# A Strassen matmul with log-sum-exp: four column blocks with the operands' roles exchanged, 512 moving columns instead of 256

## The chip, the cores and the metric

The kernel runs on one core of a Trainium2 chip. The metric is the device time of one execution in microseconds (us). Four engines matter, TensorE (PE in the profile; PEld are its weight loads), VectorE (DVE), ScalarE (ACT) and GpSimd (POOL), and the DMA queues.

## The reference

```python
m, k, n = 1024, 4096, 4096          # a: m x k, b: k x n, float32, random
x = np.matmul(a, b)
return special.logsumexp(x, axis=-1).astype(np.float32)
```

## The kernel before

Everything is cast to float16 for TensorE. A is held transposed in SBUF (`aT`). B comes in eight column blocks of 512. Block 0 is multiplied plainly while A arrives. Every other block uses one level of Strassen's scheme (in Winograd's way): a block of B is four quarters b11, b12, b21, b22, and seven products replace eight. VectorE makes the sums of quarters, T1, T4 and T6 as new tiles, T3 and T7 in place:

```python
if what == "t1":   add(self.T1[:, lo:hi], b11, b22)
elif what == "t6": add(self.T6[:, lo:hi], b11, b12)
elif what == "t4": sub(self.T4[:, lo:hi], b21, b11)
elif what == "t7": add(b21, b21, b22)
else:              sub(b12, b12, b22)                 # t3
```

T1, T4 and T6 exist once each, so the next block's T1 can be made only when TensorE has done with this block's. A block is worked off in four groups q, each of 2 x 128 rows of A. The sums of A are stationary (128 x 128), B's are moving (256 columns), and each of the seven products is 16 matmuls:

```python
def product(c, lhs, rhs, start=False, k=(0, KP)):     # KP = 16
    for i in range(*k):
        nc.tensor.matmul(c, lhs(i), rhs(i), ...)      # lhs: A's side, 128x128; rhs: B's side, 256 columns

# one group; r0, r1 are two accumulator tiles of 512 f32; c11, c12 halves of r0, c21, c22 halves of r1
s = fix_pool.tile([P, 4, H], f32, tag="s")            # scratch, one buffer
x, e = s[:, 1::2], s[:, 0:2]
m1(c11, start=True); m5(c12)
nc.scalar.copy(out=e, in_=halves(r0))                 # "the copy of e"
m2(c21, start=True); m6(c22)
nc.scalar.copy(out=s[:, 2], in_=c21)
add(s[:, 2], s[:, 2], e[:, 1]); sub(s[:, 0], s[:, 2], e[:, 0])
for f in deferred: f()
# ... sums of B for the next block ...
m3(c12); nc.scalar.copy(out=x[:, 0], in_=c12)         # "the copy of x0"
m4(c21); nc.scalar.copy(out=x[:, 1], in_=c21)
m7(c11)
sub(x, x, s[:, 0::2]); add(c22, c22, x[:, 0]); add(c11, c11, x[:, 1])
maxima()                                              # VectorE: row maxima; ScalarE: exp with a running sum, later
```

The rows of the result lie on partitions here, so the maximum of a row is one VectorE reduction, and ScalarE's exp takes it as a bias and sums as it goes.

Of the kernel before, what the change touches and what calls it, by code (L numbers as in the profile page):

```python
# [13 lines left out]
def kernel(  # L14
# [6 lines left out]
    nc = tc.nc  # L21
    P = 128
    FD = 512
    H = FD // 2
    f32 = mybir.dt.float32
    f16 = mybir.dt.float16
    AX = mybir.AxisListType
    ALU = mybir.AluOpType
    AF = mybir.ActivationFunctionType
# [4 lines left out]
    MT, KT, NB = M // P, K // P, N // FD  # L34
    MP, KP = MT // 2, KT // 2
    G = 4
    GI = KP // G
# [5 lines left out]
    cst_pool = ctx.enter_context(tc.tile_pool(name="cst", bufs=1))  # L43
    bt_pool = ctx.enter_context(tc.tile_pool(name="btp", bufs=2 * G))
    fix_pool = ctx.enter_context(tc.tile_pool(name="fix", bufs=1))
# [3 lines left out]
    psum_pool = ctx.enter_context(  # L49
        tc.tile_pool(name="psum", bufs=8, space=bass.MemoryType.PSUM)  # L50
    )
# [6 lines left out]
            name=nc.get_next_instruction_name(),  # L58
# [6 lines left out]
    aT = cst_pool.tile([P, KP, 2, MP, 2, P], f16, name="aT")  # L65
    s1 = cst_pool.tile([P, KP, MP, P], f16, name="s1")
    s2 = cst_pool.tile([P, KP, MP, P], f16, name="s2")
    s5 = cst_pool.tile([P, KP, MP, P], f16, name="s5")
    tb = cst_pool.tile([P, 3, KP, H], f16, name="tb")
    stg_slots = tb.rearrange("p t (i j) n -> p (t i) (j n)", j=4)  # L70
    NSLOT = 3 * KP // 4
    ident = cst_pool.tile([P, P], f16, name="ident")
    negmax = cst_pool.tile([P, MT, NB + 1], f32, name="negmax")
    tsum = cst_pool.tile([P, MT, NB + 1], f32, name="tsum")

# [4 lines left out]
    def add(o, x, y):  # L80
        nc.vector.tensor_tensor(out=o, in0=x, in1=y, op=ALU.add)  # L81

    def sub(o, x, y):
        nc.vector.tensor_tensor(out=o, in0=x, in1=y, op=ALU.subtract)  # L84
# [41 lines left out]

    class Block:

        def __init__(self, nb, raw=None, sums=None):
            self.nb = nb  # L130
            self.raw = raw or [
                bt_pool.tile([P, GI, 2, FD], f16, name=f"b_{nb}_{g}", tag="bt")
                for g in range(G)
            ]
            self.T1, self.T4, self.T6 = sums or (tb[:, 0], tb[:, 1], tb[:, 2])

        def load(self, lo, hi):
            nc.gpsimd.dma_start(  # L138
                out=self.raw[lo // GI][:, lo % GI : lo % GI + hi - lo],
                in_=b_rows[:, lo:hi, :, ts(self.nb, FD)],  # L140
            )
# [6 lines left out]
        def b(self, i, kp, h):  # L148
            return self.raw[i // GI][:, i % GI, kp, ts(h, H)]

        def make(self, what, lo=None, hi=None):
            if lo is None:
                for g in range(G):
                    self.make(what, g * GI, (g + 1) * GI)
                return
            u = self.raw[lo // GI][:, lo % GI : lo % GI + hi - lo]
            b11, b12 = u[:, :, 0, 0:H], u[:, :, 0, H:FD]
            b21, b22 = u[:, :, 1, 0:H], u[:, :, 1, H:FD]
            if what == "t1":
                add(self.T1[:, lo:hi], b11, b22)  # L160
            elif what == "t6":
                add(self.T6[:, lo:hi], b11, b12)
            elif what == "t4":
                sub(self.T4[:, lo:hi], b21, b11)
            elif what == "t7":
                add(b21, b21, b22)
            else:
                sub(b12, b12, b22)
# [68 lines left out]
    def a_sums_late(r, q):  # L237
        a11, a12 = aT[:, r, 0, q, 0, :], aT[:, r, 1, q, 0, :]
        a21, a22 = aT[:, r, 0, q, 1, :], aT[:, r, 1, q, 1, :]
        sub(a21, a21, a11)  # L240
        sub(a12, a12, a22)
# [97 lines left out]
    deferred = []  # L339

    def flush():
        for f in pending:
            f()
        pending.clear()
# [4 lines left out]
    again0 = lambda: Block(0, sums=[wide(t[:, :, 0:2]) for t in (s1, s2, s5)])  # L349
    again1 = lambda: Block(1, raw=[wide(aT[:, ts(g, GI), :, 0:2]) for g in range(G)])  # L350
    plan = [(lambda: blk1, range(MP - 1))]
    plan += [(lambda nb=nb: Block(nb), range(MP)) for nb in range(2, NB)]
    plan += [(again0, [MP - 1]), (again1, [MP - 1])]

    blk, nxt = None, blk1
    for step, (_, qs) in enumerate(plan):
        blk, nxt = nxt, None
        nb = blk.nb
        more = step + 1 < len(plan)
        early = more and plan[step + 1][0] is again0  # L360
        if more:
            if plan[step + 1][0] is again1:
                nxt = last
            else:
                nxt = plan[step + 1][0]()
                if step == 1:
# [3 lines left out]
                        out=ident[0:1, 0:2], in_=aT[0:1, 0, 0, MP - 1, :, 0]  # L370
# [5 lines left out]
        if step == 0:  # L376
            KH = K // 2
            for h in range(2):
                a16 = dram_pool.tile([2, P, KH], f16, name=f"a16_{h}")
                for m in range(2):  # L380
                    nc.gpsimd.dma_start(out=a16[m], in_=a_m[MT - 2 + m, :, ts(h, KH)])
                for m in range(2):
                    nc.sync.dma_start_transpose(
                        aT[:, ts(h, KP // 2), :, MP - 1, m, :].rearrange("p i t c -> p (i t) c"),
                        a16[m],
                    )
        quads = {}
        for q in qs:
            joint = step == 0
# [4 lines left out]
            c11, c12 = r0[:, 0:H], r0[:, H:FD]  # L394
            c21, c22 = r1[:, 0:H], r1[:, H:FD]

            def product(c, lhs, rhs, start=False, k=(0, KP)):
                for i in range(*k):
                    nc.tensor.matmul(  # L399
                        c,  # L400
                        lhs(i),
                        rhs(i),
                        start=(start and i == 0),
                        stop=(i == KP - 1),
                        skip_group_check=True,
                    )
# [4 lines left out]
            if final:  # L411
                c22 = psum_pool.tile([P, FD], f32, name="c22", tag="ps")[:, 0:H]
            s = fix_pool.tile([P, 4, H], f32, name=f"s_{step}_{q}", tag="s")
            x, e = s[:, 1::2], s[:, 0:2]
            if final:
                e = fix_pool.tile([P, 2, H], f32, name="e_last", tag="e")
            if joint and q > 0:
                e = e_next
# [78 lines left out]
            if final:  # L497
# [28 lines left out]
                    out=w, in_=w, func=AF.Exp, bias=n0, scale=-1.0, accum_out=l0  # L526
# [44 lines left out]
            if step == 1 and q == 1:  # L571
                a_sums_early(slice(0, KP // 2), MP - 1)
                a_sums_late(slice(0, KP // 2), MP - 1)
            if early and q == 1:
                last = again1().load_all()

    nc.sync.dma_start(out=out.rearrange("(p mt) -> p mt", mt=MT), in_=lg)
# [30 lines left out]
```

## Time and profile before

| | before |
|---|---|
| median of 20 runs | 421.94 us (421.46 to 423.25) |
| profiled span | 421.2 us |
| TensorE busy | 413.7 us (98%) |
| one Strassen block (3 to 6) | 48.9 us |
| VectorE, ScalarE busy in such a block | 26.1 us, 12.2 us |

The page of the kernel before: the span, the busy time of each engine, and the chain of work that ended last, by engine.

```profile
span 421.2 us, 8528 instructions
...
PE 413.7 (98%) x3643; PEld 348.9 (83%) x3643; DVE 258.7 (61%) x573; ACT 109.9 (26%) x279; POOL 73.0 (17%) x115
...
PE 97%; DMA 1%; DVE 0%; ACT 0%; issue 0%; SPq 0%; ACTq 0%
```

TensorE is busy nearly throughout, and it is 97% of the chain that ended last. Whatever is won must be won there, and whatever makes TensorE wait is lost.

The table by stage of the kernel before: each row is a stretch in us, then its length, and the busy time of each engine with instruction counts. The first row is block 4; the second is the first group of block 7.

```profile
core 0: us, PE busy (x) PEld busy (x) DVE busy (x) ACT busy (x) POOL busy (x), PEclk, DMA share, GB/s
...
196.78:245.69 48.91, 48.91 (x451) 43.83 (x449) 26.13 (x49) 12.20 (x32) 3.96 (x6) 1.00 0.53 87
...
343.50:355.73 12.23, 12.23 (x114) 10.96 (x113) 10.15 (x19) 3.04 (x8) 2.49 (x3) 1.00 1.15 188
```

In block 4 TensorE works for all 48.91 us, VectorE for 26.13. A group takes 12.23 us: seven products of 1.75.

How long is a matmul? The timeline of TensorE, before: start, extent, then the instruction. The extents overlap, so one reads the distance of the starts. First groups of four matmuls of 512 columns (block 0), then groups of four of 256 (block 7):

```profile
59.40 1.03 PE L221 MATMUL acc_1_94<-b_3_86,aT 128*128 128x512 f16 x4
60.26 1.03 PE L221 MATMUL acc_0_95<-b_3_86,aT 128*128 128x512 f16 x4
```

```profile
350.32 0.60 PE L399 MATMUL acc_0_0_3927<-b_0_3379,aT 128*128 128x256 f16 x4
350.76 0.60 PE L399 MATMUL acc_0_0_3927<-b_1_3380,aT 128*128 128x256 f16 x4
```

Four matmuls of 512 columns start every 0.863 us, 215.7 ns each. Four of 256 take 0.436 us, 109.1 ns each. Two of 256 columns are 2.5 ns dearer than one of 512. The Trainium skill, "TensorE: Matmul & The Clock Gate", section "Wait — 56ns, not 53.3ns?", says the same: columns at 2.4 GHz, and about 2.5 ns per matmul on top. This trace agrees (215.7 and 109.1 ns).

The timeline of VectorE, before, gives the prices for what the change puts there:

```profile
195.79 0.68 DVE L84 TENSOR_TENSOR b_1_1760<-b_1_1760 128x1024 f16<-128x1024 f16 x1
196.40 0.68 DVE L84 TENSOR_TENSOR b_2_1761<-b_2_1761 128x1024 f16<-128x1024 f16 x1
```

Operations on 1024 f16 elements start 0.60 us apart.

### The profile page before, as it was taken

What the parts mean: (1) busy time and instruction counts of PE and PEld (TensorE: products, weight loads), DVE (VectorE), ACT (ScalarE), POOL (GpSimd) and SP (SyncE); (2) the same over time, 40 slices, a digit from 0 to 9 for tenths busy, and PEclk for the clock granted to TensorE, in tenths of its full rate; (3) what the DMA queues carried; (4) which work ended last, traced back from release to release, by engine and by line L of the source; (5) the groups of instructions that cost most, each with busy time, mean ns of one, the idle gap of its engine ahead of it and who ended that gap; (6) DMA issues with size and microseconds to landing.
All of it is one profiled execution on the core that took longest, in us unless ns stands there. A gap on an engine that the chain in (4) does not pass through costs nothing.

```text
span 421.2 us, 8528 instructions
## 1 busy us (share of the span) xinstructions
PE 413.7 (98%) x3643; PEld 348.9 (83%) x3643; DVE 258.7 (61%) x573; ACT 109.9 (26%) x279; POOL 73.0 (17%) x115
## 2 busy tenths in 40 slices
PE   7999999999999999999999999999999999999995
PEld 2555558888888888888888888888888888888885
DVE  2466688878647693257812694336832587299855
ACT  2222341132132222122222212222221222222124
POOL 7667753001010020003000030000200030120000
PEclk9999999999999999999999999999999999999999
DMA  9999999999999099102990079400990039899000
GB/s 186 200 204 203 203 206 206 207 207 214 192 200 211 7 177 207 17 2 35 207 159 2 2 115 208 80 2 2 183 207 11 2 56 207 138 186 207 9 2 1
DMA packets 57845, 53.37 MB, mean 127 GB/s; under 512 B 10192, under 2 KB 56912, under 8 KB 57808
## 3 DMA queue, kind: packets, MB, share of 16 engines
q0 software_dynamic: 48928, 49.95, 71.8%
q1 hardware_dynamic: 8880, 2.89, 3.5%
q8 instruction: 28, 0.46, 0.4%
q14 instruction: 9, 0.07, 0.1%
HBM read 100.66 MB, written 2.10 MB: 244 GB/s over the span
## 4 chain that ended last, share of the span: by engine, by line
PE 97%; DMA 1%; DVE 0%; ACT 0%; issue 0%; SPq 0%; ACTq 0%
PE acc_1_92 L221 2%; PE acc_0_91 L221 2%; PE acc_0_93 L221 2%; PE acc_1_0_1343 L399 2%; PE acc_1_0_765 L399 2%; PE acc_0_0_763 L399 2%; PE acc_3_0_4335 L399 2%; PE acc_3_0_2691 L399 2%; PE acc_0_0_3927 L399 2%; PE acc_1_0_3515 L399 2%; PE acc_2_0_3103 L399 2%; PE acc_3_0_1611 L399 2%; PE acc_0_0_3387 L399 2%; PE acc_1_0_2975 L399 2%; PE acc_0_0_2307 L399 2%; PE acc_3_0_2151 L399 2%
## 5 line engine op out<-in xcount | busy, mean ns | idle before, releaser
L399 PEld LDWEIGHTS <-aT 128*128 128x128 f16 x1856 | 181.6, 98 | 21.1
L399 PEld LDWEIGHTS <-s_71 128*128 128x128 f16 x464 | 45.4, 98 | 5.5
L399 PEld LDWEIGHTS <-s_73 128*128 128x128 f16 x464 | 45.4, 98 | 5.3
L399 PEld LDWEIGHTS <-s_72 128*128 128x128 f16 x464 | 45.4, 98 | 5.3
L221 PEld LDWEIGHTS <-aT 128*128 128x128 f16 x192 | 16.7, 98 | 16.0 <-DVE aT L214 2.9
L192 POOL DMA_DIRECT2D tb<-in_a_dram x47 | 25.4, 543 | 7.0 <-issue 2.1
L203 PEld LDWEIGHTS <-tb 128*128 128x128 f16 x192 | 15.0, 100 | 12.3 <-DVE tb L296 1.0
L216 ACT COPY aT<-tps_98 128x512 f16<-128x512 f16 x24 | 14.1, 586 | 38.3 <-PE tps_98 L203 38.3
L214 DVE COPY aT<-tps_97 128x512 f16<-128x512 f16 x24 | 10.2, 424 | 19.0 <-PE tps_97 L203 19.0
L84 DVE TENSOR_TENSOR aT<-aT 128x256 f16<-128x256 f16 (+1 forms) x56 | 16.1, 339 | 0.0
L203 PE MATMUL tps_97<-ident,tb 128*128 128x128 f16 x96 | 9.5, 223 | 0.1
L203 PE MATMUL tps_98<-ident,tb 128*128 128x128 f16 x96 | 9.5, 223 | 0.0
L81 DVE TENSOR_TENSOR s_71<-aT 128x256 f16<-128x256 f16 (+1 forms) x26 | 8.1, 313 | 2.2 <-ACT aT L216 2.2
L138 POOL DMA_DIRECT2D b_0_2299<-in_b_dram x1 | 0.9, 878 | 45.9 <-PE acc_3_0_2151 L399 45.9
L138 POOL DMA_DIRECT2D b_0_3379<-in_b_dram x1 | 0.9, 878 | 45.7 <-PE acc_3_0_3231 L399 45.7
L138 POOL DMA_DIRECT2D b_0_3919<-in_b_dram x1 | 0.9, 878 | 45.1 <-PE acc_3_0_3771 L399 45.1
L138 POOL DMA_DIRECT2D b_0_2839<-in_b_dram x1 | 0.9, 890 | 45.0 <-PE acc_3_0_2691 L399 45.0
L81 DVE TENSOR_TENSOR s_72<-aT 128x256 f16<-128x256 f16 (+1 forms) x26 | 8.1, 313 | 0.0
L81 DVE TENSOR_TENSOR s_73<-aT 128x256 f16<-128x256 f16 (+1 forms) x26 | 8.1, 313 | 0.0
L138 POOL DMA_DIRECT2D aT<-in_b_dram x4 | 3.5, 897 | 21.5 <-PE acc_1_0_4055 L399 21.5
L282 PE MATMUL acc_1_96<-s_73 128*128 128x512 f16 x11 | 5.2, 608 | 1.2 <-DVE s_73 L285 1.2
L81 DVE TENSOR_TENSOR tb<-aT 128x1024 f16<-128x1024 f16 x8 | 5.2, 686 | 1.5 <-DMA aT<-in_b_dram 1.5
(1050 smaller groups left out, 891.7 us busy)
## 6 DMA issues: line engine op xcount, KB each, us to landing
tb<-in_a_dram POOLq DMA_DIRECT2D x47, 128.0 KB, 5.9
aT<-in_b_dram POOLq DMA_DIRECT2D x4, 1024.0 KB, 15.2
b_1_84<-in_b_dram POOLq DMA_DIRECT2D x4, 256.0 KB, 6.5
b_2_85<-in_b_dram POOLq DMA_DIRECT2D x4, 256.0 KB, 6.2
b_3_86<-in_b_dram POOLq DMA_DIRECT2D x4, 256.0 KB, 6.2
b_0_87<-in_b_dram POOLq DMA_DIRECT2D x2, 512.0 KB, 8.6
b_1_88<-in_b_dram POOLq DMA_DIRECT2D x2, 512.0 KB, 11.8
b_2_89<-in_b_dram POOLq DMA_DIRECT2D x2, 512.0 KB, 15.2
```

The costliest lines, as they stand in the source:

```text
L81: nc.vector.tensor_tensor(out=o, in0=x, in1=y, op=ALU.add)
L84: nc.vector.tensor_tensor(out=o, in0=x, in1=y, op=ALU.subtract)
L138: nc.gpsimd.dma_start(out=self.raw[lo // GI][:, lo % GI : lo % GI + hi - lo], in_=b_rows[:, lo:hi, :, ts(self.nb, FD)],)
L192: nc.gpsimd.dma_start(out=slot, in_=a_m[m, :, k0 * P : (k0 + kn) * P])
L203: nc.tensor.matmul(pst[:, ts(j, P)], src[:, ts(j, P)], ident, is_transpose=True, start=(j == 0), stop=(j == kn - 1),)
L214: nc.vector.tensor_copy(out=dst, in_=v)
L216: nc.scalar.copy(out=dst, in_=v)
L221: nc.tensor.matmul(pt, aT[:, i, kp, m // 2, m % 2, :], blk0.raw[i // GI][:, i % GI, kp, :], start=(done[m] == 0), stop=(done[m] == KT - 1),)
L282: nc.tensor.matmul(acc[2][1], zeros[:, 0:P], zeros[:, 0:FD], start=True, stop=True)
L399: nc.tensor.matmul(c, lhs(i), rhs(i), start=(start and i == 0), stop=(i == KP - 1), skip_group_check=True,)
```

## The change: its intent, and the diff

Blocks 3 to 6 exchange the roles: 128 columns of B's sums are stationary, and A's sums for 4 x 128 rows move, 512 columns in one matmul. A block is then two halves of 7 x 16 matmuls, not four groups of 7 x 16, so the fixed cost per matmul is paid half as often. The price is that products come out transposed: columns of the result lie on partitions, rows along the free axis. VectorE therefore turns squares of 32 x 32, takes maxima over 32 columns, subtracts them, ScalarE takes the exp, and VectorE sums. At the end GpSimd spreads the four partition groups' results into the four columns of `negmax` and `tsum` that these blocks would have filled.

```diff
+    slots = tb[:, 1, KP // 2 : KP] ...            # two scratch tiles in the unused half of T4
+    def lse_turned(c, slot, h, r):
+        nc.vector.transpose(out=slot, in_=c)
+        nc.vector.tensor_reduce(out=nm, in_=v, axis=AX.X, op=ALU.max, negate=True)
+        add(v, v, nm.unsqueeze(-1).broadcast_to((P, WN // 2, 32)))
+        nc.scalar.activation(out=slot, in_=slot, func=AF.Exp)
+        return lambda: nc.vector.tensor_reduce(out=tts[...], in_=v, axis=AX.X, op=ALU.add)
+    def merge_turned():                            # 7 small operations, one of them an exp on ScalarE
+    ...
+    def wide_step(blk, nxt):
+        for nt in range(2):
+            last = not nxt.wide and nt == 1
+            ...                                    # mk: sums for the next half, full size if last
+            product(c11, T1, s1); product(c12, b22, s5); product(c21, b11, s2)
+            nc.vector.tensor_copy(out=s[:, 1], in_=c12)
+            add(s[:, 1], s[:, 1], c21)
+            sub(s[:, 0], s[:, 1], c11)
+            for f in deferred: f()                 # end11 and merge_turned of the half before
+            mk("t1")
+            product(c22, T6, aT); mk("t6"); mk("t3")
+            product(c12, b12, aT)
+            sub(s[:, 0], c12, s[:, 0]); add(c22, c22, s[:, 0])
+            end12 = lse_turned(c12, slots[0], 1, 0)
+            end22 = lse_turned(c22, slots[1], 1, 1)
+            product(c21, T4, aT)
+            sub(s[:, 1], c21, s[:, 1])
+            end12(); end21 = lse_turned(c21, slots[0], 0, 1); end22()
+            for what in ("t4", "t7"):              # if last: only the first two quarters here
+                mk(what)
+            product(c11, b21, aT)
+            add(c11, c11, s[:, 1])
+            end11 = lse_turned(c11, e, 0, 0); end21()
+            if last: ...                           # the other two quarters of t4, t7
+            deferred.extend([end11, merge_turned])
...
+        if blk.wide:
+            wide_step(blk, nxt)
+            continue
...
+                spread_turned()                    # 32 small GpSimd copies, in block 7
                 last = again1().load_all()
```

## The prediction

> **What bounds the kernel now.** TensorE. The page gives PE 413.7 of 421.2 us (98%), and the chain of waits is 97% PE. The table by stage shows column blocks 3 to 6 at 48.9 us each, with TensorE busy throughout, VectorE 26.1 us (53%) and ScalarE 12.2 us. In the chain, 16 matmuls of 256 columns take 1.745 us, 109.1 ns each. In the timeline of the first block, four of 512 columns take 0.863 us, 215.7 ns each. That fits the Trainium skill, "TensorE: Matmul & The Clock Gate", section "Wait — 56ns, not 53.3ns?": columns at 2.4 GHz plus about 2.5 ns per matmul.
>
> **Removed from TensorE.** Each of the four blocks goes from 448 matmuls of 256 columns to 224 of 512: 896 x (2 x 109.1 - 215.7) = 2.2 us. That is the whole gain, 0.5%, all on the critical path. Weight loads (98 ns) stay hidden.
>
> **Added on VectorE.** ScalarE's copies and its summing exp move here. I price with starts in the VectorE timeline: 1024 f16 or 512 f32 elements 0.60 us back to back, 256 cycles 0.334 us (0.067 us fixed), about 0.12 us more when the operation reads its predecessor's result. For each half block (TensorE needs 112 x 215.7 ns = 24.2 us):
> - 20 block sums at half size, 0.334 each: 6.7
> - copy, add, sub of the first products and four combines: 4.7
> - four squares turned (transpose, max, subtract): 4 x 2.04 = 8.2. I take the transpose as one element per cycle (skill, "Vector Engine (DVE) Microarchitecture Reference", section 3.8); no trace here shows one yet.
> - four final sums: 2.4
> - merge, seven small operations with a trip to ScalarE: 1.75
>
> Estimate: 23.7 us of 24.2, against about 13 before. VectorE goes to 95-100% in these blocks. TensorE has 2 to 4 us of slack there (tightest: the copy of the second product before its bank is used again), so little or no stall.
>
> **Where I expect the loss: leaving the wide blocks.** The last half of block 6 makes full-size sums for block 7 (5.3 us more) with VectorE already full and about 10 us behind. Block 7's first group reuses the scratch tile, which frees only when VectorE's last combine is done. ScalarE, in order, first runs the last exp, then copies; only then may TensorE write that bank again; T4 and T7 arrive late too. By my sum TensorE stalls 4 to 8 us there. After that VectorE recovers. The 32 tiny POOL copies, 0.1 to 0.3 us each, precede block 1's reload, and may cost 0 to 2 us.
>
> **Sum.** 421.7 - 2.2 + 5 (exit) + 0.5 (rest) = 425 us. Range 418 to 437. Chances: faster by over 2% 0.01, within 2% 0.78, slower by over 2% 0.21.
>
> **What would show it.**
> - Timeline: 512-column matmuls 215.7 ns apart in blocks 3 to 6, four blocks at about 193.3 us instead of 195.6.
> - Table by stage: VectorE over 90% there; before, 53%.
> - Groups: transpose of 128x512 f32 near 0.7 us. Wrong if over 1 us.
> - Waits: one TensorE gap of several us at the start of block 7, released by ScalarE's copy or a VectorE sum; hardly any between wide halves.
> - The end after block 7 costs as before, within 2 us.
>
> **What would make it wrong.** A transpose at half rate adds some 2 us per half, ending near 435 to 440. If dependent VectorE steps cost less than priced, VectorE is not behind at the exit, the stall shrinks to 1 or 2 us, and the time is 420 to 421. A moving operand in four pieces of 128 columns could stream slower; I assume not.

## The result, and the profile after

The changed kernel takes 427.82 us in the median of 10 runs (426.82 to 428.94), against 421.94. The ratio is 1.0137, 95% interval 1.0126 to 1.0148: 1.4% slower. (Ratios are the mean time of one kernel's runs over that of the other's of the same rounds, so not quite the ratio of the medians.) The result is correct.

The page after: span, busy times, TensorE's busy tenths and its granted clock in 40 slices, and the chain.

```profile
span 426.6 us, 6832 instructions
...
PE 413.0 (97%) x2747; PEld 261.3 (61%) x2747; DVE 338.3 (79%) x773; ACT 83.3 (20%) x191; POOL 79.1 (19%) x149
...
PE   7999999999999999999999999999999958999996
...
PEclk9999999999999999999999999999999996999999
...
PE 88%; DVE 6%; DMA 4%; ACT 1%; issue 0%; SPq 0%; ACTq 0%
```

TensorE's busy time is almost what it was, but one slice shows 5 and its neighbour 8, and the clock falls to 6 tenths in the second of them. Those slices are the start of block 7.

The table by stage after (columns as above): block 4, the first group of block 7, and the piece of it that follows TensorE's wait.

```profile
195.19:243.53 48.34, 48.34 (x225) 21.94 (x224) 45.85 (x99) 5.65 (x11) 3.96 (x5) 1.00 0.54 89
...
340.23:361.41 21.18, 15.20 (x114) 12.39 (x113) 18.17 (x34) 4.18 (x9) 4.12 (x18) 0.84 1.18 196
353.19:359.66 6.47, 6.46 (x34) 4.71 (x34) 4.40 (x13) 0.77 (x3) 1.29 (x9) 0.55 1.24 207
```

A wide block takes 48.34 us where 48.91 stood, with TensorE busy throughout. Four of them take 193.39 us instead of 195.63, that is 2.24 less. VectorE is busy for 45.85 of 48.34 us, 95%. The first group of block 7 takes 21.18 us where 12.23 stood: 8.95 more. In the part behind TensorE's wait the granted clock is 0.55. (Block 3, the first wide one, has VectorE busy for only 39.3 us, 81%.)

So in the profiles: 2.24 won in the wide blocks, 8.95 lost at the exit, and 1.04 less before block 2 starts (97.85 against 98.89 us), in a part that the change hardly touches and whose length differs from run to run; the end after that group takes 65.19 against 65.47 us. Together 5.4, the difference of the two spans.

The waits of TensorE after, with their total, count and longest in us: the only one over 1.2.

```profile
PE acc_0_0_3173 L528 <- ACT s_0_3175 L595: 6.0, 1, 6.0
```

L595 is the copy of `e`. The timeline of TensorE around it:

```profile
345.30 1.91 PE L528 MATMUL acc_0_1_3174<-tb,aT 128*128 128x256 f16 x16
353.19 1.01 PE L528 MATMUL acc_0_0_3173<-b_0_2813,aT 128*128 128x256 f16 x4 [5.98 <-ACT s_0_3175 L595]
...
356.56 3.10 PE L528 MATMUL acc_0_1_3174<-tb,aT 128*128 128x256 f16 x16
359.50 0.60 PE L528 MATMUL acc_0_0_3173<-b_0_2813,aT 128*128 128x256 f16 x4
...
361.24 1.91 PE L528 MATMUL acc_1_0_3307<-tb,s_71 128*128 128x256 f16 x16
```

The product m3 (at 353.19) starts 6.0 us after m6, the product before it, has ended. Then its 16 matmuls take 3.37 us (353.19 to 356.56), where 16 took 1.75 before: half the speed, through m3 and most of m4. At 359.50, with m7, the speed is back. These two products take 6.31 us instead of 3.49: 2.82 us, besides the 5.98 of the wait.

The timeline of VectorE at the exit:

```profile
349.06 0.69 DVE L86 TENSOR_TENSOR wide_1_0_2993<-wide_1_0_2993,sw_1_2997 128x512 f32<-128x512 f32 x1
...
351.26 0.69 DVE L86 TENSOR_TENSOR ew_1_3155<-ew_1_3155,ident 128x512 f32<-128x512 f32 x1
...
354.39 0.69 DVE L86 TENSOR_TENSOR b_3_2816<-b_3_2816 128x1024 f16<-128x1024 f16 x1
354.99 0.42 DVE L86 TENSOR_TENSOR s_0_3175<-s_0_3175 128x256 f32<-128x256 f32 x1
```

The add at 349.06 is the last combine of block 6 (it frees the scratch tile), the one at 351.26 the last subtraction ahead of ScalarE's last exp. The line at 354.39 finishes T7; T4 was finished just before. At 354.99 comes VectorE's first add of block 7, which before came 8.2 us after the block's start (351.72 against 343.50); the block began at 340.2, so it now comes 14.8 after.

The timeline of ScalarE at the exit:

```profile
352.04 0.63 ACT L381 ACTIVATE ew_1_3155<-ew_1_3155 128x512 f32<-128x512 f32 x1 [5.24 <-DVE ew_1_3155 L86]
352.58 0.57 ACT L595 COPY s_0_3175<-acc_0_0_3173 128x512 f32<-128x512 f32 x1
...
356.96 0.28 ACT L391 ACTIVATE ident<-ident 128x96 f32<-128x96 f32 x1 [3.54 <-DVE ident L89]
357.15 0.35 ACT L670 COPY s_0_3175<-acc_0_0_3173 128x256 f32<-128x256 f32 x1
```

ScalarE works in program order: the exp of block 6's last square (352.04), then the copy of `e` (352.58), which sets m3 free. Later the exp of the merge (356.96), then the copy of x0 (357.15).

Inside the wide blocks there is no TensorE gap. The timeline of VectorE there, with its only wait of a half for TensorE, and a transpose:

```profile
229.76 0.69 DVE L86 TENSOR_TENSOR sw_1_2293<-sw_1_2293,wide_1_2_2291 128x512 f32<-128x512 f32 x1 [0.41 <-PE wide_1_2_2291 L427]
...
240.70 0.71 DVE L378 STREAM_TRANSPOSE tb<-wide_1_3_2292 128x512 f32<-128x512 f32 x1
```

VectorE waits 0.41 us for the third product in a half of 24.2 us. The transpose of 128 x 512 f32 takes 0.71 us.

### The profile page after: what moved, and what is told of

It is laid out like the page before. It is cut to its first block, busy times and chain, and to the rows that moved or that the text cites. A ratio compares the mean times of both kernels' runs of the same rounds, so it can differ in the third digit from the quotient of the medians.

```text
span 426.6 us, 6832 instructions
## 1 busy us (share of the span) xinstructions
PE 413.0 (97%) x2747; PEld 261.3 (61%) x2747; DVE 338.3 (79%) x773; ACT 83.3 (20%) x191; POOL 79.1 (19%) x149
## 4 chain that ended last, share of the span: by engine, by line
PE 88%; DVE 6%; DMA 4%; ACT 1%; issue 0%; SPq 0%; ACTq 0%
DMA tb<-in_a_dram 3%; PE acc_1_0_1347 L528 2%; PE acc_1_0_767 L528 2%; PE acc_0_0_765 L528 2%; PE acc_2_0_3483 L528 2%; PE acc_2_0_1482 L528 2%; PE acc_1_0_3307 L528 2%; PE acc_3_0_3755 L528 2%; PE acc_3_0_3619 L528 2%; PE acc_3_0_1615 L528 2%; PE acc_0_0_1215 L528 2%; PE acc_2_0_769 L528 2%; PE wide_0_1_2822 L427 2%; PE wide_1_2_2643 L427 2%; PE wide_0_0_2469 L427 2%; PE wide_1_1_2290 L427 2%
## 5 line engine op out<-in xcount | busy, mean ns | idle before, releaser
L528 PEld LDWEIGHTS <-aT 128*128 128x128 f16 x832 | 82.8, 100 | 17.1 <-issue 6.2
L427 PEld LDWEIGHTS <-tb 128*128 128x128 f16 x384 | 37.6, 98 | 45.1
L381 ACT ACTIVATE tb<-tb 128x512 f32<-128x512 f32 x24 | 15.1, 630 | 110.4 <-DVE tb L86 110.4
L234 PEld LDWEIGHTS <-aT 128*128 128x128 f16 x192 | 16.6, 98 | 14.4 <-DVE aT L227 1.8
L216 PEld LDWEIGHTS <-tb 128*128 128x128 f16 x192 | 13.9, 98 | 14.3 <-DMA tb<-in_a_dram 6.2
L528 PEld LDWEIGHTS <-s_71 128*128 128x128 f16 x208 | 20.4, 98 | 2.8
L528 PEld LDWEIGHTS <-s_73 128*128 128x128 f16 x208 | 20.4, 98 | 2.3
L528 PEld LDWEIGHTS <-s_72 128*128 128x128 f16 x208 | 20.3, 98 | 2.4
L86 DVE TENSOR_TENSOR tb<-tb,ident 128x512 f32<-128x512 f32 x24 | 16.6, 692 | 0.8
L379 DVE TENSOR_REDUCE ident<-tb 128x16 f32<-128x512 f32 x24 | 16.5, 686 | 0.9
L382 DVE TENSOR_REDUCE tts<-tb 128x16 f32<-128x512 f32 x24 | 16.2, 677 | 0.0
L86 DVE TENSOR_TENSOR s_71<-aT 128x256 f16<-128x256 f16 (+1 forms) x26 | 8.1, 313 | 2.1 <-ACT aT L229 1.5
```

What stands on the lines that cost most here:

```text
L86: nc.vector.tensor_tensor(out=o, in0=x, in1=y, op=ALU.add)
L216: nc.tensor.matmul(pst[:, ts(j, P)], src[:, ts(j, P)], ident, is_transpose=True, start=(j == 0), stop=(j == kn - 1),)
L234: nc.tensor.matmul(pt, aT[:, i, kp, m // 2, m % 2, :], blk0.raw[i // GI][:, i % GI, kp, :], start=(done[m] == 0), stop=(done[m] == KT - 1),)
L379: nc.vector.tensor_reduce(out=nm, in_=v, axis=AX.X, op=ALU.max, negate=True)
L381: nc.scalar.activation(out=slot, in_=slot, func=AF.Exp)
L382: return lambda: nc.vector.tensor_reduce(out=tts[:, 1 + h, ts(r, WN // 2)], in_=v, axis=AX.X, op=ALU.add)
```

## The experiments

The theory (A): VectorE is so full in the wide blocks that it enters block 7 with a queue; TensorE waits there, once, for what the queue holds back; the lowered clock is a consequence of that wait. Rivals: the loss belongs to the wide blocks themselves; or one single dependence makes it. "First group" below is from the first matmul of the first group behind the wide blocks to the first of the next group, from the profile of that run; 12.23 us before.

| run | median us | ratio to before, 95% | first group us |
|---|---|---|---|
| the change | 427.82 | 1.0137 (1.0126 to 1.0148) | 21.2 |
| e1_warm | 426.91 | 1.0111 (1.0095 to 1.0127) | 19.2 |
| e2_order | 426.20 | 1.0094 (1.0079 to 1.0109) | 19.3 |
| e3_scratch | 427.52 | 1.0144 (1.0106 to 1.0181) | 21.2 |
| e4_both | 428.10 | 1.0147 (1.0124 to 1.0170) | 20.6 |
| e11_order_and_merge | 425.25 | 1.0067 (1.0052 to 1.0083) | 17.6 |
| e7_two_together | 428.49 | 1.0154 (1.0140 to 1.0168) | 20.2 |
| e6_two_apart | 437.66 | 1.0361 (1.0344 to 1.0379) | 21.0 and 20.9 |
| e8_dose_inside | 428.60 | 1.0150 (1.0134 to 1.0165) | 21.0 |
| e10_dose_inside_big | 431.57 | 1.0221 (1.0205 to 1.0236) | 23.3 |
| e9_dose_exit | 430.43 | 1.0197 (1.0182 to 1.0213) | 22.4 |
| e5_late_squares | 419.76 | 0.9943 (0.9930 to 0.9955) | 12.2 |

All were correct. e1 to e4 ran on one chip, e5 to e11 on another, each beside its own runs of the kernel before (422.0 and 422.1 us).

### e1_warm: does the clock drop come from the idle time?

```diff
+            if nb == NB - 1 and q == 0:
+                idle = psum_pool.tile([P, FD], f32, name="idle", tag="ps")
+                for _ in range(24):                   # 512 columns each, result unused
+                    nc.tensor.matmul(idle..., aT[:, 0, 0, 0, 0, :], s1[:, 0], start=True, stop=True)
             m3(c12)
```

> 24 idle 512-column matmuls (24 x 215.7 ns = 5.2 us) are put where TensorE waits at the start of block 7. Theory A (the wait is set by VectorE's queue and ScalarE's order; the clock drop after it is a consequence of the idle time): the third product of block 7 still starts about 13.1 us after the block's start, since the fillers end before that; but the two products after the gap run at 109 ns per matmul and not 184 to 210, so block 7's first group takes about 18.2 us and not 21.2, and the run is 2.5 to 3 us shorter than the changed kernel: about 425. Rival B (those two products are slow for another cause, late sums or a busy memory): the time stays at 427.8, within 0.6.

Measured: 426.91 us. The timeline of TensorE in this run (fillers, m3, m4, m7):

```profile
347.29 5.34 PE L672 MATMUL idle<-s,aT 128*128 128x512 f16 x24
353.44 1.91 PE L528 MATMUL acc<-b,aT 128*128 128x256 f16 x16 [0.81 <-ACT s L595]
355.18 1.91 PE L528 MATMUL acc<-tb,aT 128*128 128x256 f16 x16
357.80 1.91 PE L528 MATMUL acc<-b,aT 128*128 128x256 f16 x16 [0.71 <-ACT s L680]
```

With the array kept busy, m3 still starts 13.1 us into the block, but runs at full speed (1.74 us from 353.44 to 355.18), and the granted clock of the whole run is 1.000 against 0.992. So the clock drop was a consequence of idle time: this half of the expectation held. The size was missed: about 1 us was saved, not 2.5 to 3. The last product shows why. It stands behind a new wait, 0.71 us, for a copy by ScalarE. ScalarE's timeline in this run:

```profile
357.20 0.28 ACT L391 ACTIVATE ident<-ident 128x96 f32<-128x96 f32 x1 [3.54 <-DVE ident L89]
357.39 0.35 ACT L680 COPY s<-acc 128x256 f32<-128x256 f32 x1
```

The copy of x0 (357.39) stands behind the exp of the merge (357.20), which waits for VectorE's queue. In the changed kernel the slow products had hidden this wait. The Trainium skill, "TensorE: Matmul & The Clock Gate", section "HAM oscillation — how this bites in real kernels", describes the drop: idle time longer than a window of about 3.4 us halves the clock until TensorE has been busy for a while. The 6.0 us wait of the changed kernel and the doubled durations after it agree; e2's wait of 3.3 us lies at the edge, and e4 below does not fit.

### e2_order and e3_scratch: which link holds m3?

Two edits, each alone. e2 issues ScalarE's last exp of block 6 behind the copies of block 7:

```diff
-        nc.scalar.activation(out=slot, in_=slot, func=AF.Exp)
+        exp = lambda: nc.scalar.activation(out=slot, in_=slot, func=AF.Exp)
+        if later is not None: later.append(exp)      # later = deferred, for the last square only
+        else: exp()
```

> Only ScalarE's last exp of block 6 is issued after the two copies of block 7. Theory A, with the exp ahead of the copy as the link that ends last: the copy now starts when the scratch tile comes free, about 9.6 us into block 7 and not 12.4, so TensorE's first gap falls from 6.0 to about 3.2 us; then it waits again for T4's and T7's last quarters (VectorE finishes them about 14.9 us into the block): the group takes about 16.5 us if the clock stays full, 18 to 19 if it drops; the run is 423 to 425.5. Rival (scratch tile or T4 and T7 alone set the gap): no change, 427.8 within 0.6.

e3 makes VectorE's last combine of block 6 earlier, so that the scratch tile comes free sooner:

```diff
             sub(s[:, 1], c21, s[:, 1])
+            if last:
+                product(c11, ...)
+                add(c11, c11, s[:, 1])
             end12()
```

> Only VectorE's last combine of block 6, which frees the scratch tile, is moved ahead of the third square: the tile comes free some 5.5 us sooner. Theory A: ScalarE's last exp still stands ahead of the copy, so TensorE's gap stays 6.0 us within 0.6 and the run 427.8 within 0.7. Rival (the scratch tile sets the gap): gap near zero, a wait for T4 instead, and 423 to 425.

Measured: e3 changed nothing (427.52 us, TensorE's wait 6.0 us, first group 21.2): the scratch tile alone was not what ended last. (Its profile is of the one execution of four that took 430.70 us; block 7 starts 2.4 us later there than in the change, so that excess lies before it.) e2 shortened the first wait from 6.0 to 3.3 us, as expected, but 3.3 us still brought the slow clock for the whole of m3, and a second wait of 1.8 us came behind m4. TensorE's timeline (m3 and m7):

```profile
350.36 3.57 PE L532 MATMUL acc<-b,aT 128*128 128x256 f16 x16 [3.27 <-ACT s L599]
...
357.44 1.91 PE L532 MATMUL acc<-b,aT 128*128 128x256 f16 x16 [1.77 <-ACT s L674]
```

Its 426.20 us is above the 423 to 425.5 expected: I had the link to m3 right. The second wait was not the one for T4 and T7 that I expected: m4 did not wait, and m7 waited for the copy of x0, a link that I had not seen.

### e4_both

Both edits together.

> Both of the former together. Theory A: TensorE's gap before the third product vanishes, and a gap of 3.5 to 4 us before the second half of the fourth product takes its place, since T4's last two quarters wait for the third and fourth squares (their memory is the squares' scratch): 422.5 to 423.5 if the clock stays full, up to 425.5 if it drops. Rival (only ScalarE's order or the tile counted): 419 to 420.

Measured: 428.10 us, no better than the change alone, and outside what either theory had said. TensorE's timeline (m3, first and second half of m4, m7, the next group):

```profile
348.54 1.91 PE L536 MATMUL acc<-b,aT 128*128 128x256 f16 x16 [0.92 <-DVE tb L89]
350.28 1.04 PE L536 MATMUL acc<-tb,aT 128*128 128x256 f16 x8
353.80 1.80 PE L536 MATMUL acc<-tb,aT 128*128 128x256 f16 x8 [2.48 <-DVE tb L89]
358.03 3.21 PE L536 MATMUL acc<-b,aT 128*128 128x256 f16 x16 [2.43 <-ACT s L678]
361.07 1.91 PE L536 MATMUL acc<-tb,s 128*128 128x256 f16 x16
```

The first wait is down to 0.92 us, where none was expected, and the one for T4 is there (2.48 us, where 3.5 to 4 was expected). But m7 again waits for the copy of x0 (2.43 us) and starts 17.6 us into the block, against 17.5 in e1 and e2. In all these versions m7 starts where VectorE's queue and the merge let it. Worse, the clock dropped, though no single wait was longer than 2.5 us. The second half of m4, behind waits of 0.92 and 2.48 us, has an extent of 1.80 us for 8 matmuls where its first half has 1.04; the granted clock there is 0.51. The same happens in m7 behind the third wait (3.04 us for 16, from 358.03 to 361.07).

### e11_order_and_merge: the link to m7

e2 with the exp of the last merge, too, moved behind block 7's copies of x0 and x1.

```diff
             nc.scalar.copy(out=x[:, 1], in_=c21)
+            while after_copies: after_copies.pop()()      # exp of the merge, and the rest of it
```

> The kernel with only ScalarE's last exp put behind the copies, and now the exp of the merge as well put behind block 7's later copies. Theory A with a fourth link (the last product of block 7's first group waits for ScalarE's copy of the fourth bank half, which stands behind the merge's exp, and that waits for VectorE's queue to end): TensorE's second gap falls from 1.8 us to about 0.5, since the copy can start when VectorE's first add of block 7 is done, 15.3 us into the block; the run is 1 to 1.6 us shorter than with the one exp moved, 424.6 to 425.3. Rival (that copy waits for something other than the merge's exp): the second gap stays, 426.2 within 0.5.

Measured: 425.25 us, 0.95 less than e2 in the medians; the two ran on different chips, and by the ratios the difference is 1.1 us, sure to about 0.9. TensorE's timeline, m3 and m7:

```profile
351.48 3.18 PE L541 MATMUL acc<-b,aT 128*128 128x256 f16 x16 [3.28 <-ACT s L608]
...
356.92 1.91 PE L541 MATMUL acc<-b,aT 128*128 128x256 f16 x16
```

The second wait is gone (0.5 us was expected), and m7 starts 15.9 us into the block instead of 17.5. So the merge's exp ahead of the copy was that link. The copy of x0 now waits for VectorE's first add of block 7, which stands behind T7. The wait of 3.3 us before m3, and the slow clock behind it, remain.

### e7_two_together and e6_two_apart: per block, or per exit?

Only two wide blocks, next to each other (3, 4), or apart (3, 5). The statistics get two more columns, and `d` moves into memory that is free by then, to fit.

```diff
-    WIDE = range(3, NB - 1)
+    WIDE = (3, 4)                       # e7;  (3, 5) in e6
+    COLS = list(WIDE) + list(range(NB, NC))
```

> Only blocks 3 and 4 are wide, one exit (into block 5). Theory A (the loss is per exit, the gain 0.56 us per wide block): 422.0 - 1.1 + 8.9 less what a start takes by chance: 428 to 430.5, more than the changed kernel with four wide blocks. Rival (the loss grows with the number of wide blocks, since VectorE falls behind a little in each): 424.5 to 426.

> Blocks 3 and 5 are wide, two exits (into blocks 4 and 6). Theory A: twice the exit: 422.0 - 1.1 + 2 x 8.9 = 438.7, within 436 to 440. Rival (loss by wide blocks): as with two wide blocks together, 424.5 to 430.

Measured: 428.49 and 437.66 us, both as theory A said. Two wide blocks together cost as much as four (0.7 us more by the ratios, sure to about 0.8); the same two blocks apart cost 9.2 us more. TensorE's waits for the copy of `e` with two exits: total, count, longest.

```profile
PE acc L530 <- ACT s L597: 12.0, 2, 6.1
```

The loss is per exit from wide to narrow, and doesn't grow with the number of wide blocks.

### e8, e10 and e9: the same VectorE work, inside or at the exit

VectorE repeats one maximum of 512 columns (0.72 us each, result unchanged): three times more in the second half of block 3 (e8), seven times more there (e10), three times more in the last half of block 6 (e9).

```diff
-        nc.vector.tensor_reduce(out=nm, in_=v, axis=AX.X, op=ALU.max, negate=True)
+        for _ in range(times):
+            nc.vector.tensor_reduce(out=nm, in_=v, axis=AX.X, op=ALU.max, negate=True)
```

> The same 2.2 us of extra VectorE work as in the exit dose, but in the second half of the first wide block. Theory A: inside the wide blocks VectorE idles 0.35 to 0.4 us in each half, before it adds the third product, and TensorE has over 3 us of slack there: the six halves that follow take up about 2.3 us, no TensorE gap inside, and the time is 427.8 within 0.8. Rival (VectorE at its limit all through the wide blocks, so that any work added is paid): 430, as with the dose at the exit.

> The dose inside, raised to 7 x 0.72 = 5.0 us. Theory A: about 2.3 us are taken up by the idle time of the six halves that follow; the rest, 2.7 us, is paid: a part as a TensorE gap of about 1 us in the half after the dose, where the copy of the second product now comes later than 13.8 us into the half, the rest at the exit: 429.6 to 431.5. Rival (the slack is per half and nothing carries over to the exit): 428 to 429.

> In the last wide half VectorE does one 512-column maximum four times instead of once: 3 x 0.72 = 2.2 us more work, the result unchanged. Theory A: all of it is paid: 427.8 + 2.2 = 430, within 429.3 to 431. Rival (the exit is set by something other than VectorE's queue): 427.8 within 0.7.

Measured against the change (differences of the ratios to before, times 422 us): 2.2 us of work inside cost 0.5 us; the same 2.2 us at the exit cost 2.5; 5.0 us inside cost 3.5. Each of these differences is sure to about 0.8 us. So inside the wide blocks VectorE's spare 0.4 us per half took up about 1.6 us of either dose, somewhat less than the 2.3 expected; what goes beyond that is paid. TensorE's wait for the copy of `e` says the same: 6.0 us in the change, 6.5 in e8, 8.2 in e9. (The first group grew by only 1.2 us in e9, since the slow clock behind the wait ended sooner in the execution that was profiled, the fastest of the four.) With the big dose TensorE waits inside as well, once, in the half after it:

```profile
PE acc L529 <- ACT s L596: 8.2, 1, 8.2
PE wide L428 <- DVE sw L442: 1.4, 1, 1.4
```

e8 and e9 fell within what theory A expected (e8 at its upper edge); the big dose, expected at 429.6 to 431.5, measured 431.57, just outside. VectorE is thus at its limit in the wide blocks, but with slack enough that only the exit pays in the kernel as it stands.

### e5_late_squares: the exit cleared

In the last wide half VectorE first does what block 7 needs; the last two squares are turned later, where VectorE has time.

```diff
             sub(s[:, 1], c21, s[:, 1])
+            if last:
+                product(c11, ...)
+                add(c11, c11, s[:, 1])            # frees the scratch tile
+                end12(); end22()                  # frees T4's second half
+                mk("t4")
+                deferred.append(lambda: nxt.make("t7"))      # behind block 7's first add
+                def squares():                    # behind block 7's first maxima
+                    exps = []
+                    ends = [lse_turned(c11, e, 0, 0, exps), lse_turned(c21, c22, 0, 1, exps)]
+                    deferred.extend(exps + ends + [lambda: merge_turned(split=True)])
+                after_maxima.append(squares)
+                continue
...
-                spread_turned()
                 last = again1().load_all()
+                spread_turned()
```

The exps stand behind the copies of block 7's second group; the merge's exp stands behind that group's copies of x0 and x1, and its last four operations are GpSimd's. c21's square is turned into c22's accumulator tile, which is free by then.

> The way out of the wide blocks is cleared of everything that TensorE does not need: in the last half VectorE does the fourth combine right after the third, then T4, T7 after block 7's first add; the last two squares are turned behind block 7's first maxima, their exps stand behind the copies of the next group, the merge is ended on GpSimd. Theory A (VectorE's queue at the exit is the whole loss, TensorE's gain stands): block 7's first group takes 12.2 to 13.5 us and not 21.2, no drop of the clock, VectorE still over 90% busy in the wide halves, and the run is 419.2 to 420.5, 0.3 to 0.6% below the kernel before. Rival (a VectorE that full costs time elsewhere too, or the delayed squares stall a later group): 421.5 or more.

Measured: 419.76 us, ratio 0.9943 (0.9930 to 0.9955). It beats both kernels: 0.6% below the kernel before, 1.9% below the change by the ratios. The timelines of TensorE (block 7's start, m3, m7, next group) and of ScalarE (copies of `e` and of x0):

```profile
339.72 1.91 PE L549 MATMUL acc<-tb,s 128*128 128x256 f16 x16
...
346.70 1.91 PE L549 MATMUL acc<-b,aT 128*128 128x256 f16 x16
...
350.20 1.91 PE L549 MATMUL acc<-b,aT 128*128 128x256 f16 x16
351.94 1.91 PE L549 MATMUL acc<-tb,s 128*128 128x256 f16 x16
```

```profile
343.90 0.59 ACT L616 COPY s<-acc 128x512 f32<-128x512 f32 x1 [0.83 <-DVE wide L86]
...
348.65 0.37 ACT L691 COPY s<-acc 128x256 f32<-128x256 f32 x1 [1.37 <-PE acc L549]
```

The products follow each other at 1.745 us, with no wait and no slow clock; the group takes 12.22 us as in the kernel before. The wide blocks take 193.39 us, and VectorE is busy there for 176.9 us, as in the change (176.8). Its load there is unchanged; what differs is the order at the exit, and that GpSimd ends the merge. The edit moves several pieces of work at once, and no run shows which of them could have stayed.

## Why the prediction was right or wrong

The measured 427.82 us lies within the stated 418 to 437, in the class given most weight (within 2%), 2.8 us above the 425 named.

- TensorE's gain, 2.2 us: measured 2.24 (193.39 against 195.63). Right. The moving operand in four pieces of 128 columns did stream at 215.7 ns per matmul.
- VectorE at 95 to 100% in the wide blocks: measured 95% busy in blocks 4 to 6, with one wait of 0.35 to 0.41 us per half for a product. Right there; block 3, which starts without a queue, had 81%. The transpose, priced at one element per cycle as in the skill's "Vector Engine (DVE) Microarchitecture Reference", section 3.8, took 0.70 to 0.72 us.
- No TensorE wait inside the wide blocks: right. A dose of 2.2 us (e8) still made none, one of 5.0 us (e10) made a wait of 1.4, so TensorE's slack lay between the two doses; 2 to 4 us was stated.
- One TensorE wait at the start of block 7, released by ScalarE's copy behind the last exp: right, line for line; 6.0 us, within the 4 to 8 stated. e6 and e7 show that the loss belongs to the exit, e5 that clearing the exit returns all of it.
- The size of the exit's term was off. The sum had 5 us; the first group cost 8.95 more. The missing part is mostly the clock (the wait itself was 1 us longer than the 5): I took the wait itself as the cost, and left out that TensorE came back from it at half the granted clock, which cost 2.82 us in the next two products. The page on TensorE that I cited for the matmul's price describes such a drop after idle time, too.
- Not seen at all: the fourth link, the copy of x0 behind the merge's exp. In the changed kernel the slow clock hides it; e1 and e11 brought it out. For that reason the clock's 2.82 us could not be recovered alone: e1 got back about 1.
- T4 and T7 late: they were, but m3 waited longer for the copy. TensorE waits for T4 only in e4, and for T7 in no run.
- GpSimd's 32 copies: 0.19 us each, 6.3 us in all, done before block 1's reload could start. Cost 0, as the low end said.
- "Rest, 0.5": the start came out about 1 us shorter in the profile, and the end after block 7's first group 0.28 shorter; nothing in the runs ties either to the change. By the profiles this made up for part of the exit's error: the exit term was 3.95 us too low, the sum ended only 2.8 too low. That much of the agreement is luck.

## What to carry to other kernels

When a change loads a helper engine to 95%, look for the loss not inside the steady stretch but where it ends: there the queue meets work that needs the engine at once, and each exit pays once. Freeing one link of such a queue changed nothing (e3) or moved the wait to the next link (e2, e4); reordering the whole queue by what the bottleneck needs first returned everything (e5). And price a long wait of TensorE with the slow matmuls behind it: here m3 and m4 took 1.8 us (e7) to 2.8 us (the change) longer behind waits of 6.0.

## What the Trainium skill lacked or had wrong

- "TensorE: Matmul & The Clock Gate", section "Why this matters for your kernels", asks for no idle gap above about 3 us between bursts, and its Part 1 speaks of a window of about 3.4 us. A wait of 3.3 us, at this limit, brought the slow clock (e2). In e4 waits of 0.92 and 2.48 us, with 24 matmuls at full speed between them, brought it too (granted clock 0.51 behind the second), though neither reaches the limit. Two waits of 0.8 and 0.7 us did not (e1). The page says in "A second HAM failure mode: psum-queue depth-cycling" that frequent short idle times can do this, but gives no lengths for them.
- The same page, section "Back-to-back issue gap", gives about 131 ns per matmul of 512 columns as the sustained rate with weight loads, and says that N/2.4 + 2.5 over-counts there. 512 columns with a weight load before each took 215.7 ns throughout, before and after, and 256 columns 109.1 ns: the formula fits and the 131 was not seen.
- "VectorE: DVE Perf Modes", section "The three transpose paths", has VectorE's transpose only for 128 x 128 bf16. From an f32 accumulator, 128 x 512, it took 0.70 to 0.72 us in these runs, about as long as the other operations on 512 f32 elements (0.68 to 0.70), which fits one element per cycle in "Vector Engine (DVE) Microarchitecture Reference", section 3.8. The table also has no VectorE transpose into an accumulator; e5 made one, in 0.72 us, with a correct result.
- No page says what a full VectorE or ScalarE queue does to the first work behind it; here it cost 8.95 us at one point of a kernel whose steady part lost nothing.
